# An absolute-difference row sum on one core: seven neighbouring rows and one distant row per partition, two stores, and all instructions in the first block

## The chip, the cores and the metric

One core of one Trainium2 chip. The time is device microseconds of the whole program, median of several executions. Where a ratio is given, it is the mean time of one kernel's fast runs over the mean of the other kernel's fast runs of the same rounds, so it is not quite the ratio of the medians that stand beside it. "Landing" below always means the last of the semaphore updates of a DMA (16 for most), as the trace records it.

In the lines of the profile DVE is VectorE, ACT is ScalarE and SP is SyncE, which issues most of the DMAs; a "q" after the name marks work of the engine's sequencer (waits, branches, the issue of DMAs), and L131 is line 131 of the kernel. A DMA moves its data in packets (2160 in the trace of the kernel before). The "first block" is the stretch of instructions that an engine runs before the framework's first jump.

## The reference

```python
def setup_inputs():
    batch, dim = 1024, 4096
    return {"x": np.random.randn(batch, dim).astype(np.float32),
            "y": np.random.randn(batch, dim).astype(np.float32), "axis": -1}

def reference(x, y, axis):
    return np.sum(np.abs(x - y), axis=axis).astype(np.float32)
```

Two inputs of 16.8 MB are read and 1024 sums (4 KB) are written. The sums are all alike: for these inputs their mean is 4623 and their standard deviation 57. So a kernel that stores right sums in a wrong order passes the comparison.

## The kernel before

A partition holds eight neighbouring rows, so it reads 128 KB in one piece of memory and its neighbour starts 128 KB further on. The first four rows of x and y come in two large DMAs that are issued at entry. The next three rows of x follow, then the y rows one by one as VectorE frees their buffers, and the eighth row in four shrinking pieces. VectorE subtracts, ScalarE takes the absolute value and sums. The eight sums of a partition are neighbours in the output too: one store of 32 bytes per partition.

```python
xr = x.rearrange("(p k) c -> p k c", p=P, k=K)          # K = 8: pitch 8 x 16 KB = 128 KB
orr = out.rearrange("(p k) -> p k", p=P, k=K)
...
at_entry(nc, lambda: nc.sync.dma_start(out=xa, in_=xr[:, 0:H, :]).then_inc(early[0], 16), "Drain")
at_entry(nc, lambda: nc.scalar.dma_start(out=yb, in_=yr[:, 0:H, :]).then_inc(early[1], 16), "Drain")
nc.sync.dma_start(out=xb[:, 0:H - 1, :], in_=xr[:, H:K - 1, :])
...                                                      # (cut: the work on rows 0 to 6)
else:                                                    # the last of the four pieces
    nc.vector.tensor_sub(out=last[:, n_part:n_part + w], in0=tx[:, s], in1=ty[:, s])
    nc.vector.reduce_sum(out=ro[:, K - 1:K], in_=last, axis=AX, apply_absolute_value=True)
...
nc.sync.dma_start(out=orr, in_=ro)                       # 32 bytes per partition
```

## Time and profile before

| | before |
|---|---|
| time, median (lowest to highest) | 86.28 us (86.19 to 86.42), 3 runs |
| span of the profiled run | 84.54 us |
| loads: first packet starts, last one ends | 1.00, 80.19 us |
| first block landed, first subtract | 41.49, 41.80 us |
| last piece landed, last reduce starts | 80.68, 81.53 us |
| store issued, landed | 82.11, 83.53 us: 1.42 us |
| landing of the store to the end of the span | 1.02 us |

How to read it: the 16 DMA engines are busy from 1 to 80 us, and what follows the last landing (80.68) is a tail of 3.86 us: a subtract, a reduce, a store, and the framework's exit.

```profile
out_dram<-ro SPq DMA_DIRECT2D x1, 4.0 KB, 1.4
```

The store of all 4 KB takes 1.4 us; SyncE, which has 0.35 us of issuing to do itself, waits for 1.1 of it.

### The profile page before, as it was taken

What the parts mean: (1) busy time and instruction counts of PE and PEld (TensorE: products, weight loads), DVE (VectorE), ACT (ScalarE), POOL (GpSimd) and SP (SyncE); (2) the same over time, 40 slices, a digit from 0 to 9 for tenths busy, and PEclk for the clock granted to TensorE, in tenths of its full rate; (3) what the DMA queues carried; (4) which work ended last, traced back from release to release, by engine and by line L of the source; (5) the groups of instructions that cost most, each with busy time, mean ns of one, the idle gap of its engine ahead of it and who ended that gap; (6) DMA issues with size and microseconds to landing.
All of it is one profiled execution on the core that took longest, in us unless ns stands there. A gap on an engine that the chain in (4) does not pass through costs nothing.

```text
span 84.5 us, 110 instructions
## 1 busy us (share of the span) xinstructions
DVE 36.5 (43%) x15; ACT 31.2 (37%) x25; POOL 0.2 (0%) x4
## 2 busy tenths in 40 slices
DVE  0000000000000000000299999999298997988860
ACT  5000000000000000000001979797971968999950
POOL 0000000000000000000000000000000000000000
DMA  9479999995799999957999888999999999999700
GB/s 496 186 310 496 496 496 496 496 465 217 310 496 496 496 496 496 465 217 310 512 581 395 372 372 372 411 450 411 457 403 450 419 394 421 421 407 402 290 0 2
DMA packets 2160, 33.56 MB, mean 397 GB/s; under 512 B 368, under 2 KB 624, under 8 KB 1392
## 3 DMA queue, kind: packets, MB, share of 16 engines
q1 hardware_dynamic: 2016, 25.17, 70.8%
q10 hardware_dynamic: 144, 8.39, 22.9%
HBM read 33.55 MB, written 0.00 MB: 397 GB/s over the span
## 4 chain that ended last, share of the span: by engine, by line
DMA 67%; DVE 16%; ACT 13%; issue 1%; ACTq 0%; DVEq 0%
DMA yb_rows<-in_y_dram 67%; DVE xa_rows L64 10%; DVE xb L64 5%; ACT xb L85 5%; ACT xb L65 4%; ACT xb L95 4%; DVE ro L98 1%; ACTq L131 0%; DVEq L131 0%; DVEq L68 0%
## 5 line engine op out<-in xcount | busy, mean ns | idle before, releaser
L64 DVE TENSOR_TENSOR xa_rows<-xa_rows,yb_rows 128x4096 f32<-128x4096 f32 x4 | 17.4, 4420 | 41.8 <-DMA yb_rows<-in_y_dram 41.8
L65 ACT ACTIVATE xa_rows<-xa_rows 128x4096 f32<-128x4096 f32 x4 | 14.5, 3617 | 45.9 <-DVE xa_rows L64 45.9
L64 DVE TENSOR_TENSOR xb<-xb,yb_rows 128x4096 f32<-128x4096 f32 x2 | 8.9, 4426 | 2.0 <-DMA yb_rows<-in_y_dram 2.0
L65 ACT ACTIVATE xb<-xb 128x4096 f32<-128x4096 f32 x2 | 7.2, 3617 | 3.4 <-DVE xb L64 3.4
L84 DVE TENSOR_TENSOR xb<-xb,yb_rows 128x1024 f32<-128x1024 f32 (+1 forms) x3 | 4.6, 1576 | 0.5 <-DMA yb_rows<-in_y_dram 0.5
L94 DVE TENSOR_TENSOR xb<-xb,yb_rows 128x1984 f32<-128x1984 f32 (+2 forms) x3 | 4.3, 1447 | 0.9 <-DMA yb_rows<-in_y_dram 0.9
L85 ACT ACTIVATE xb<-xb 128x1024 f32<-128x1024 f32 (+1 forms) x3 | 4.0, 1323 | 0.0
L95 ACT ACTIVATE xb<-xb 128x1984 f32<-128x1984 f32 (+2 forms) x3 | 3.7, 1229 | 0.0
L65 ACT ACT_TABLE_LOAD x1 | 1.3, 1283 | 0.9 <-PEq L117 0.9
L65 ACT ACTIVATION_READ_ACCUMULATOR xa_rows<-xa_rows 128x1 f32 x4 | 0.7, 186 | 0.0
L98 DVE TENSOR_REDUCE ro<-last 128x1 f32<-128x387 f32 x1 | 0.6, 556 | 0.2 <-ACT xb L95 0.2
L97 DVE TENSOR_TENSOR last<-xb,yb_rows 128x384 f32<-128x384 f32 x1 | 0.6, 558 | 0.1
L95 ACT ACTIVATION_READ_ACCUMULATOR xb<-xb 128x1 f32 x3 | 0.6, 187 | 0.0
L85 ACT ACTIVATION_READ_ACCUMULATOR xb<-xb 128x1 f32 x3 | 0.6, 185 | 0.0
L65 ACT ACTIVATION_READ_ACCUMULATOR xb<-xb 128x1 f32 x2 | 0.4, 186 | 0.0
L92 DVE TENSOR_REDUCE ro<-part 128x1 f32<-128x3 f32 x1 | 0.2, 156 | 0.2 <-ACT xb L85 0.2
L117 POOL MEMSET const-bfloat16-1.0<- 128x1 bf16 x1 | 0.1, 101 | 0.0
L117 POOL MEMSET const-uint8-127<- 128x1 uint8 x1 | 0.1, 101 | 0.0
L117 POOL MEMSET const-float32-0.0<- 128x1 f32 x1 | 0.1, 98 | 0.2 <-issue 0.2
L117 POOL MEMSET const-float32-1.0<- 128x1 f32 x1 | 0.1, 98 | 0.0
## 6 DMA issues: line engine op xcount, KB each, us to landing
xb<-in_x_dram SPq DMA_DIRECT2D x1, 6144.0 KB, 54.9
yb_rows<-in_y_dram SPq DMA_DIRECT2D x3, 2048.0 KB, 15.0
xb<-in_x_dram SPq DMA_DIRECT2D x1, 992.0 KB, 17.6
yb_rows<-in_y_dram SPq DMA_DIRECT2D x1, 992.0 KB, 16.1
xb<-in_x_dram SPq DMA_DIRECT2D x1, 544.0 KB, 17.1
yb_rows<-in_y_dram SPq DMA_DIRECT2D x1, 544.0 KB, 17.9
xb<-in_x_dram SPq DMA_DIRECT2D x1, 320.0 KB, 18.3
yb_rows<-in_y_dram SPq DMA_DIRECT2D x1, 320.0 KB, 18.6
```

The costliest lines, as they stand in the source:

```text
L64: nc.vector.tensor_sub(out=tx, in0=tx, in1=ty)
L65: nc.scalar.activation(tx, tx, ABS, accum_out=ro[:, k:k + 1])
L84: nc.vector.tensor_sub(out=tx, in0=tx, in1=ty)
L85: nc.scalar.activation(tx, tx, ABS, accum_out=part6[:, i:i + 1])
L92: nc.vector.reduce_sum(out=ro[:, K - 2:K - 1], in_=part6, axis=AX)
L94: nc.vector.tensor_sub(out=tx[:, s], in0=tx[:, s], in1=ty[:, s])
L95: nc.scalar.activation(tx[:, s], tx[:, s], ABS, accum_out=last[:, i:i + 1])
L97: nc.vector.tensor_sub(out=last[:, n_part:n_part + w], in0=tx[:, s], in1=ty[:, s])
L98: nc.vector.reduce_sum(out=ro[:, K - 1:K], in_=last, axis=AX, apply_absolute_value=True)
L117: nc = _bacc.Bacc("TRN2", target_bir_lowering=False, num_devices=1)
```

## The change

The intent, as I read it from the code: partitions 112 KB apart, not a power of two; no framework between the instructions, each wait on one own semaphore; no jump to a second block. The price of the layout: the last 128 rows are a block of their own, one row per partition, so their sums are 128 neighbouring floats and need a store of their own.

```diff
-    xr = x.rearrange("(p k) c -> p k c", p=P, k=K)
-    orr = out.rearrange("(p k) -> p k", p=P, k=K)
+    M = (K - 1) * P
+    xr = x[0:M, :].rearrange("(p k) c -> p k c", p=P, k=K - 1)
+    orr = out[0:M].rearrange("(p k) -> p k", p=P, k=K - 1)
+    xl, yl, ol = x[M:R, :], y[M:R, :], out[M:R].rearrange("(p k) -> p k", p=P, k=1)
...  # every instruction goes through put(), which moves it into the first block
-        for sem in early:
-            at_entry(nc, lambda: nc.vector.wait_ge(sem, 16), "UnconditionalBranch")
+    for k in range(H):
+        sub(xa[:, k, :], yb[:, k, :], [(s_first, 32)] if k == 0 else [])
...
-        nc.sync.dma_start(out=orr, in_=ro)
+    put(lambda: nc.sync.wait_ge(s_row7, 1))
+    put(lambda: nc.sync.wait_ge(s_piece[-1], 32))
+    put(lambda: nc.sync.dma_start(out=orr, in_=ro[:, 0:K - 1]).then_inc(s_out, 16))
+    put(lambda: nc.sync.wait_ge(s_end, n_part + 2))
+    put(lambda: nc.sync.dma_start(out=ol, in_=ro[:, K - 1:K]).then_inc(s_out, 16))
+    put(lambda: nc.sync.wait_ge(s_out, 32))
```

More of the change, by code (lines that the diff above doesn't have):

```diff
@@ L9, with __init__, put @@
 AX = mybir.AxisListType.X
+F32 = mybir.dt.float32
+ABS = mybir.ActivationFunctionType.Abs
+AX = mybir.AxisListType.X
 PIECES = [1984, 1088, 640, 384]
 ROW6 = [2048, 1024, 1024]
-def at_entry(nc, emit, before):
-    hook = nc.inst_callbacks[-1]
-    lower = nc._always_lower_symbolic_ap
-    nc.remove_inst_callback(hook)
-    nc._always_lower_symbolic_ap = False
-    try:
-        ins = emit().ins
-    finally:
-        nc._always_lower_symbolic_ap = lower
-        nc.push_inst_callback(hook)
-    here = nc.cur_bb.bb.instructions
-    main = nc.main_func.blocks[0].instructions
-    at = [i for i, x in enumerate(here) if x.name == ins.name]
-    assert len(at) == 1
-    mine = here.pop(at[0])
-    first = next(i for i, x in enumerate(main) if x.engine == mine.engine and x.opcode == before)
-    main.insert(first, mine)
+class Entry:
+    def __init__(self, nc):
+        self.nc = nc
+    def put(self, emit, early=False):
+        nc = self.nc
+        hook = nc.inst_callbacks[-1]
+        lower = nc._always_lower_symbolic_ap
+        nc.remove_inst_callback(hook)
+        nc._always_lower_symbolic_ap = False
+        here = nc.cur_bb.bb.instructions
+        n = len(here)
+        try:
+            emit()
+        finally:
+            nc._always_lower_symbolic_ap = lower
+            nc.push_inst_callback(hook)
+        here = nc.cur_bb.bb.instructions
+        main = nc.main_func.blocks[0].instructions
+        before = "Drain" if early else "UnconditionalBranch"
+        while len(here) > n:
+            mine = here.pop(n)
+            first = next(i for i, x in enumerate(main) if x.engine == mine.engine and x.opcode == before)
+            main.insert(first, mine)
 @with_exitstack
@@ L40 @@
     K = R // P
-    xr = x.rearrange("(p k) c -> p k c", p=P, k=K)
-    yr = y.rearrange("(p k) c -> p k c", p=P, k=K)
-    orr = out.rearrange("(p k) -> p k", p=P, k=K)
-    assert sum(PIECES) == C
+    M = (K - 1) * P
+    xr = x[0:M, :].rearrange("(p k) c -> p k c", p=P, k=K - 1)
+    yr = y[0:M, :].rearrange("(p k) c -> p k c", p=P, k=K - 1)
+    orr = out[0:M].rearrange("(p k) -> p k", p=P, k=K - 1)
+    xl, yl, ol = x[M:R, :], y[M:R, :], out[M:R].rearrange("(p k) -> p k", p=P, k=1)
+    assert sum(PIECES) == C and sum(ROW6) == C
     n_part = len(PIECES) - 1
@@ L47 @@
     H = K // 2
-    ps = ctx.enter_context(tc.tile_pool(name="ps", bufs=1))
-    with tc.manual_schedule():
-        xa = nc.alloc_sbuf_tensor("xa_rows", [P, H, C], F32).ap()
-        xb = ps.tile([P, H, C], F32, tag="xb")
-        yb = nc.alloc_sbuf_tensor("yb_rows", [P, H, C], F32).ap()
-        ro = ps.tile([P, K], F32, tag="ro")
-        part6 = ps.tile([P, n6], F32, tag="part6")
-        last = ps.tile([P, n_part + PIECES[-1]], F32, tag="last")
-        early = [tc.alloc_semaphore("early_x"), tc.alloc_semaphore("early_y")]
-        at_entry(nc, lambda: nc.sync.dma_start(out=xa, in_=xr[:, 0:H, :]).then_inc(early[0], 16), "Drain")
-        at_entry(nc, lambda: nc.scalar.dma_start(out=yb, in_=yr[:, 0:H, :]).then_inc(early[1], 16), "Drain")
-        nc.sync.dma_start(out=xb[:, 0:H - 1, :], in_=xr[:, H:K - 1, :])
-        def whole(tx, ty, k):
-            nc.vector.tensor_sub(out=tx, in0=tx, in1=ty)
-            nc.scalar.activation(tx, tx, ABS, accum_out=ro[:, k:k + 1])
-        for sem in early:
-            at_entry(nc, lambda: nc.vector.wait_ge(sem, 16), "UnconditionalBranch")
-        for k in range(H):
-            whole(xa[:, k, :], yb[:, k, :], k)
-            if k < H - 1:
-                nc.sync.dma_start(out=yb[:, k, :], in_=yr[:, H + k, :])
-                continue
-            o = 0
-            for w in PIECES:
-                nc.sync.dma_start(out=xb[:, k, o:o + w], in_=xr[:, K - 1, o:o + w])
-                nc.sync.dma_start(out=yb[:, k, o:o + w], in_=yr[:, K - 1, o:o + w])
-                o += w
-        for k in range(H - 2):
-            whole(xb[:, k, :], yb[:, k, :], H + k)
-        o = 0
-        for i, w in enumerate(ROW6):
-            tx, ty = xb[:, H - 2, o:o + w], yb[:, H - 2, o:o + w]
-            nc.vector.tensor_sub(out=tx, in0=tx, in1=ty)
-            nc.scalar.activation(tx, tx, ABS, accum_out=part6[:, i:i + 1])
-            o += w
-        tx, ty = xb[:, H - 1, :], yb[:, H - 1, :]
-        o = 0
-        for i, w in enumerate(PIECES):
-            s = slice(o, o + w)
-            if i == 1:
-                nc.vector.reduce_sum(out=ro[:, K - 2:K - 1], in_=part6, axis=AX)
-            if i < n_part:
-                nc.vector.tensor_sub(out=tx[:, s], in0=tx[:, s], in1=ty[:, s])
-                nc.scalar.activation(tx[:, s], tx[:, s], ABS, accum_out=last[:, i:i + 1])
-            else:
-                nc.vector.tensor_sub(out=last[:, n_part:n_part + w], in0=tx[:, s], in1=ty[:, s])
-                nc.vector.reduce_sum(out=ro[:, K - 1:K], in_=last, axis=AX, apply_absolute_value=True)
-            o += w
-        nc.sync.dma_start(out=orr, in_=ro)
@@ new lines, with sbuf @@
+    put = Entry(nc).put
+    def sbuf(name, shape):
+        return nc.alloc_sbuf_tensor(name, shape, F32).ap()
+    xa = sbuf("xa_rows", [P, H, C])
+    xb = sbuf("xb_rows", [P, H, C])
+    yb = sbuf("yb_rows", [P, H, C])
+    ro = sbuf("ro_sums", [P, K])
+    part6 = sbuf("part6_sums", [P, n6])
+    last = sbuf("last_piece", [P, n_part + PIECES[-1]])
+    s_first = tc.alloc_semaphore("s_first")
+    s_xb = tc.alloc_semaphore("s_xb")
+    s_row = [tc.alloc_semaphore(f"s_row{k}") for k in range(H - 1)]
@@ new lines @@
+    s_piece = [tc.alloc_semaphore(f"s_piece{i}") for i in range(len(PIECES))]
+    s_sub = tc.alloc_semaphore("s_sub")
+    s_act = tc.alloc_semaphore("s_act")
+    s_end = tc.alloc_semaphore("s_end")
+    s_row7 = tc.alloc_semaphore("s_row7")
+    s_out = tc.alloc_semaphore("s_out")
+    put(lambda: nc.sync.dma_start(out=xa, in_=xr[:, 0:H, :]).then_inc(s_first, 16), early=True)
+    put(lambda: nc.scalar.dma_start(out=yb, in_=yr[:, 0:H, :]).then_inc(s_first, 16), early=True)
+    put(lambda: nc.sync.dma_start(out=xb[:, 0:H - 1, :], in_=xr[:, H:K - 1, :]).then_inc(s_xb, 16))
@@ new lines @@
+    for k in range(H - 1):
+        put(lambda: nc.sync.wait_ge(s_sub, k + 1))
+        put(lambda: nc.sync.dma_start(out=yb[:, k, :], in_=yr[:, H + k, :]).then_inc(s_row[k], 16))
+    o = 0
+    for i, w in enumerate(PIECES):
+        c = slice(o, o + w)
+        put(lambda: nc.sync.dma_start(out=xb[:, H - 1, c], in_=xl[:, c]).then_inc(s_piece[i], 16))
+        if i == 0:
+            put(lambda: nc.sync.wait_ge(s_sub, H))
+        put(lambda: nc.sync.dma_start(out=yb[:, H - 1, c], in_=yl[:, c]).then_inc(s_piece[i], 16))
+        o += w
@@ new lines, with sub, absum @@
+    count = [0, 0]
+    def sub(tx, ty, waits):
+        for s, v in waits:
+            put(lambda: nc.vector.wait_ge(s, v))
+        put(lambda: nc.vector.tensor_sub(out=tx, in0=tx, in1=ty).then_inc(s_sub, 1))
+        count[0] += 1
+    def absum(tx, to, sem):
+        put(lambda: nc.scalar.wait_ge(s_sub, count[0]))
+        put(lambda: nc.scalar.activation(tx, tx, ABS, accum_out=to).then_inc(sem, 1))
+        count[1] += sem is s_act
+    for k in range(H):
+        sub(xa[:, k, :], yb[:, k, :], [(s_first, 32)] if k == 0 else [])
+        absum(xa[:, k, :], ro[:, k:k + 1], s_act)
@@ new lines @@
+    for k in range(H - 2):
+        sub(xb[:, k, :], yb[:, k, :], ([(s_xb, 16)] if k == 0 else []) + [(s_row[k], 16)])
+        absum(xb[:, k, :], ro[:, H + k:H + k + 1], s_act)
+    o = 0
+    for i, w in enumerate(ROW6):
+        c = slice(o, o + w)
+        sub(xb[:, H - 2, c], yb[:, H - 2, c], [(s_row[H - 2], 16)] if i == 0 else [])
+        absum(xb[:, H - 2, c], part6[:, i:i + 1], s_act)
+        o += w
+    done6 = count[1]
+    o = 0
+    for i, w in enumerate(PIECES):
+        c = slice(o, o + w)
+        tx, ty = xb[:, H - 1, c], yb[:, H - 1, c]
+        if i == 1:
+            put(lambda: nc.vector.wait_ge(s_act, done6))
+            put(lambda: nc.vector.reduce_sum(out=ro[:, K - 2:K - 1], in_=part6, axis=AX).then_inc(s_row7, 1))
+        if i < n_part:
+            sub(tx, ty, [(s_piece[i], 32)])
+            absum(tx, last[:, i:i + 1], s_end)
+        else:
+            put(lambda: nc.vector.wait_ge(s_piece[i], 32))
+            put(lambda: nc.vector.tensor_sub(out=last[:, n_part:n_part + w], in0=tx, in1=ty).then_inc(s_end, 1))
+            put(lambda: nc.vector.wait_ge(s_end, n_part + 1))
+            put(lambda: nc.vector.reduce_sum(out=ro[:, K - 1:K], in_=last, axis=AX, apply_absolute_value=True).then_inc(s_end, 1))
+        o += w
```

## The prediction

> **What bounds the kernel now.** I read the page first (engine shares, the 40 slices), then the chain that ended last, then windows cut where the load changes, then the timeline of the end, and last the single records of the trace (DMA packets, semaphore instructions), which the page leaves out. The page says that no compute engine is the bound: VectorE 43%, ScalarE 37%, while the DMA row is at nine tenths or more nearly throughout.
>
> ```profile
> DVE 36.5 (43%) x15; ACT 31.2 (37%) x25; POOL 0.2 (0%) x4
> ```
>
> The chain of waits, in order of time, shows the same: two long stretches are DMA, and only the last 19 us are compute.
>
> ```profile
> 0.13 41.36 DMA yb_rows<-in_y_dram
> ...
> 41.80 8.77 DVE xa_rows L64 x2
> ...
> 50.59 15.02 DMA yb_rows<-in_y_dram
> 65.61 0.02 issue
> 65.63 4.44 DVE xb L64
> 70.07 0.02 issue
> 70.09 3.71 ACT xb L65 x2
> 73.80 3.97 ACT xb L85 x6
> 77.77 3.63 ACT xb L95 x5
> 81.40 0.10 ACTq L131
> ```
>
> The reader is to see that the chain leaves the DMA at 65.61, when row 5 lands, and that ScalarE then never rests from 70.09 to 81.5. But the loads go on beside it, and their rate is in the windows (window in us, its length, busy time of DVE, ACT and POOL, clock, DMA share, GB/s):
>
> ```profile
> 1.00:4.00 3.00, 0.00 (x0) 1.20 (x1) 0.00 (x0) 1.00 1.05 350
> 4.00:40.00 36.00, 0.00 (x0) 0.00 (x0) 0.00 (x0) 1.00 1.01 437
> ...
> 42.00:55.00 13.00, 13.00 (x4) 7.49 (x5) 0.00 (x0) 1.00 1.00 432
> 55.00:70.00 15.00, 13.02 (x3) 11.05 (x6) 0.00 (x0) 1.00 0.99 424
> 70.00:78.00 8.00, 7.00 (x6) 7.91 (x9) 0.00 (x0) 1.00 1.01 414
> ```
>
> From 4 us on all 16 DMA engines are busy without a gap. The packet records say how: the first packet starts at 1.00 us, the last load packet ends at 80.19, the last piece has landed at 80.68. Each of the 128 packets of 65,536 bytes of the first y block took 2418 or 2420 ns, which is 27.1 GB/s for one engine and 433.7 for 16. The 16,384-byte packets took 611 ns, the 1,536-byte ones 67; that is about 10 ns a packet beside the bytes. Only the very first packet of each engine differs: 2775 to 3632 ns. The engine of the 3632 ns packet begins its second at 4.638, the next slowest at 4.467; and at every later landing the sixteenth engine is about 0.2 us behind the fifteenth (last piece: 80.49, 80.68).
>
> The end of the timeline shows how both limits meet:
>
> ```profile
> 80.66 0.74 ACT L95 ACTIVATE xb<-xb 128x640 f32<-128x640 f32 x1
> 80.77 0.56 DVE L97 TENSOR_TENSOR last<-xb,yb_rows 128x384 f32<-128x384 f32 x1
> 81.31 0.19 ACT L95 ACTIVATION_READ_ACCUMULATOR xb<-xb 128x1 f32 x1
> 81.53 0.56 DVE L98 TENSOR_REDUCE ro<-last 128x1 f32<-128x387 f32 x1 [0.19 <-ACT xb L95]
> 82.11 0.35 SPq L100 DMA_DIRECT2D out_dram<-ro  x1
> ```
>
> The last subtract ends at 81.33 (a DMA end), ScalarE's last sum at 81.49: 0.16 us apart, and both hang on landings (80.68 and 65.61). So an earlier load stream moves the end by as much; a shorter ScalarE alone by at most 0.16. Then come the store (82.11, landed 83.53) and the exit: four semaphore waits of SyncE at 83.54, 83.61, 83.67 and 83.74, two drains at 83.81 and 83.86, a barrier, a clear, a second barrier, to 84.54. The timed run was 86.32, so 1.78 us lie outside the span; I take them as constant.
>
> [...] the 128 packets of the store take 7 to 9 ns each and run from 82.95 to 83.15, yet it lands 1.42 us after issue. [...] with one wait, the row-5 subtract starts 0.02 us after the landing (65.61, 65.63); with two, the row-4 one 0.09 after (60.71, 60.80).
>
> **The change part by part.**
>
> Pitch 112 KB. Bytes (33.55 MB), packet sizes (64, 48, 16 KB, then the four pieces) and their order on the queue stay. One engine moves 2,097,152 bytes at 27.1 GB/s: 77.4 us plus some 10 ns for each packet[...]. What is open is the first packet: 2775 to 3632 where 2418 is steady, so 0.4 to 1.2 us of start-up[...]. If the new addresses spare the slow engine its extra, its stream moves 4.638 - 4.467 = 0.17 us forward; if all came to the level of the median first packet (about 4.26 for the second packet's start), 0.38. I take -0.25. It lies on the path to both ends (rows 5 and the last piece land earlier), so it counts in full.
>
> The last row as a block of its own (pitch 16 KB): the packets keep their sizes of 7936 to 1536 bytes, so 302 to 67 ns each: 0.
>
> First block, waits joined. Before, VectorE starts at 41.80 though the last landing was 41.49: a semaphore instruction at 41.51, then a branch at 41.59 that carried the other wait. With one semaphore counted to 32 on the subtract it should start near 41.51: 0.28 us earlier. This is not on the path: the second-block y rows are issued at 46.25 but their packets start only at 54.79, behind the x block in the queue. Worth 0. Likewise one wait per piece, not two, spares some 0.07 us each: the 640 subtract ends 0.07 earlier, and ScalarE's last piece, which starts at 80.66 because of it, could start at 80.54 + 0.09 = 80.63. -0.03. The table load of ScalarE (1.28 us) may end up behind its first wait; ScalarE idles 0.63 + 0.62 + 0.63 + 2.29 + 1.12 = 5.29 us between 46 and 70, so 0.
>
> Two stores. The first (28 bytes a partition) goes when the last piece has landed, 80.7; SyncE needs 0.35 us for it and is free at 81.1, before the 82.1 of the second. The second moves 4 bytes a partition, not 32, [...] 1.42 again, with something for 128 four-byte writes into the same 512 bytes. +0.1.
>
> Exit. The four semaphore waits go, since the framework tracks no DMA any more: 83.805 - 83.542 = 0.26. In their place the wait for the stores sits on a branch; a branch cost SyncE about 0.06 at entry (0.85 to 0.915). -0.2.
>
> Sum: -0.25 - 0.03 + 0.1 - 0.2 = -0.38, so 86.28 becomes 85.9.
>
> **The rivals.** First, the pitch matters for the whole stream, and loads become several per cent faster. For: the diff goes to the trouble of a second store for it. Against: [...] the GB/s dips of the page's slices (186, 217) are only large packets counted by where they fall, as the even windows show. It would need 1.7 us[...]. Second, the pitch does nothing at all[...]: then -0.13, 86.15. Third, the four-byte store is slow[...]: +0.5 to +1.0 on the path, which eats all gains, 86.3 to 86.9. Against it: 32-byte writes [...] landed in 1.42. Fourth, ScalarE takes over as the bound once loads are earlier: its chain of 11.4 us from 70.09 hangs on row 5's landing, which moves with the stream, so it gains the same; no loss. Fifth, [...] the branch on VectorE took 0.21 to its next instruction; +0.1.
>
> **Range and chances.** With the first packets between -0.5 and 0, the store between 0 and +0.4, the exit between -0.3 and 0, the time lies between 85.4 and 86.4 (8 in 10: the extremes seldom meet, and three runs before spanned 0.23). Two per cent is 1.73 us, under 84.55 or over 88.01; nothing in the working reaches either. Faster 0.03, within 2% 0.95, slower 0.02.
>
> **What would show it.** Right: steady packets again of 2418 ns; first packets with a maximum below 3.4 us; the first landing near 41.2, the last piece near 80.4; first subtract 0.02 us after its landing; no run of four waits after the last store; second store landing 1.4 to 1.6 us after issue. Wrong: steady packets other than 2418; a last store over 1.8 us; ScalarE's last sum more than 0.3 us behind the last subtract; or a change in the 1.78 us outside the span.

The sum: it came to -0.38, so 85.9. That more than the first packets' excess could not be gained rested on a limit of the load rate; it was my assumption then, and not shown. The +0.1 for the second store and the +0.5 to +1.0 of the third rival were guesses: no trace gave a number for them.

## More of the kernel before

The lines are shown in the prediction. Two more, which matter for the result: SyncE's waits (who waited for whom, us in total, times, longest) and the row of the DMA issues (KB, us from issue to landing).

```profile
SPq L131 <- DMA out_dram<-ro: 1.1, 1, 1.1
```

## The result, and the profile after

The changed kernel takes **94.47 us** (93.83 to 95.06, 6 runs) against 86.25 (86.19 to 86.53, 6 runs). The ratio is 1.0943, with a 95% interval of 1.0893 to 1.0993. The profiled run was 94.11 us with a span of 92.33.

The chain of waits ends with the last compute instruction, and up to there hardly anything has changed (start us, us, what):

```profile
0.12 41.77 DMA yb_rows<-in_y_dram
41.90 0.02 issue
...
66.06 4.44 DVE xb_rows L109
70.49 0.02 issue
70.52 11.37 ACT xb_rows L114 x13
81.89 0.10 ACTq L184
81.99 0.02 issue
82.02 0.56 DVE ro_sums L144
```

The last reduce starts at 82.02 where it was 81.53: half a microsecond of the eight. The rest comes after it, where the windows show that nothing is busy at all:

```profile
4.00:40.00 36.00, 0.00 (x0) 0.00 (x0) 0.00 (x0) 1.00 1.01 437
...
81.00:83.70 2.70, 1.24 (x3) 0.98 (x4) 0.00 (x0) 1.00 0.06 2
83.70:91.40 7.70, 0.00 (x0) 0.00 (x0) 0.00 (x0) 1.00 0.00 0
```

No engine works from 83.7 to 91.4, nor does a DMA engine have a packet. What the program waits for stands in SyncE's waits and in the DMA issues:

```profile
SPq L184 <- DMA out_dram<-ro_sums: 8.4, 1, 8.4
```

```profile
out_dram<-ro_sums SPq DMA_DIRECT2D x1, 3.5 KB, 1.5
out_dram<-ro_sums SPq DMA_DIRECT2D x1, 0.5 KB, 8.8
```

The store of 3.5 KB lands in 1.5 us, near the 1.4 of the one before; the one of 0.5 KB takes 8.8. Its packets are not slow: the packet records show 128 of 4 bytes, 7 to 9 ns each, begun between 83.44 and 83.63. But the 16 semaphore updates come one by one from 87.76 to 91.39.

The whole difference adds up from the records:

| stretch | before | after | difference |
|---|---|---|---|
| start to issue of the last store | 82.11 | 82.60 | +0.49 |
| last store, issue to landing | 1.42 | 8.79 | +7.37 |
| its landing to the end of the span | 1.02 | 0.93 | -0.08 |
| span | 84.54 | 92.33 | +7.78 |

### The profile page after: what moved, and what is told of

It reads as the page before. It is cut to its first block, busy times and chain, and to the rows that moved or that the text cites. A ratio compares the mean times of both kernels' runs of the same rounds, so it can differ in the third digit from the quotient of the medians.

```text
span 92.3 us, 100 instructions
## 1 busy us (share of the span) xinstructions
DVE 36.5 (39%) x15; ACT 31.3 (34%) x25; POOL 0.2 (0%) x4
## 4 chain that ended last, share of the span: by engine, by line
DMA 62%; DVE 15%; ACT 12%; issue 0%; ACTq 0%
DMA yb_rows<-in_y_dram 62%; ACT xb_rows L114 12%; DVE xa_rows L109 10%; DVE xb_rows L109 5%; DVE ro_sums L144 1%; ACTq L184 0%
## 5 line engine op out<-in xcount | busy, mean ns | idle before, releaser
L109 DVE TENSOR_TENSOR xb_rows<-xb_rows,yb_rows 128x4096 f32<-128x4096 f32 (+5 forms) x8 | 17.8, 2241 | 3.6 <-DMA yb_rows<-in_y_dram 3.6
L114 ACT ACTIVATE xb_rows<-xb_rows 128x4096 f32<-128x4096 f32 (+5 forms) x8 | 14.9, 1863 | 3.7 <-DVE xb_rows L109 3.7
L114 ACT ACTIVATION_READ_ACCUMULATOR xb_rows<-xb_rows 128x1 f32 x8 | 1.5, 188 | 0.0
L144 DVE TENSOR_REDUCE ro_sums<-last_piece 128x1 f32<-128x387 f32 x1 | 0.6, 556 | 0.2 <-ACT xb_rows L114 0.2
L142 DVE TENSOR_TENSOR last_piece<-xb_rows,yb_rows 128x384 f32<-128x384 f32 x1 | 0.6, 559 | 0.1
```

The costliest lines, as they stand in the source:

```text
L109: put(lambda: nc.vector.tensor_sub(out=tx, in0=tx, in1=ty).then_inc(s_sub, 1))
L114: put(lambda: nc.scalar.activation(tx, tx, ABS, accum_out=to).then_inc(sem, 1))
L142: put(lambda: nc.vector.tensor_sub(out=last[:, n_part:n_part + w], in0=tx, in1=ty).then_inc(s_end, 1))
L144: put(lambda: nc.vector.reduce_sum(out=ro[:, K - 1:K], in_=last, axis=AX, apply_absolute_value=True).then_inc(s_end, 1))
```

## The experiments

My theory after the two traces: the 4-byte writes are slow because 128 of them crowd into 512 bytes. The rivals: a 4-byte write is slow anywhere; the second store is held up by the first or by the shared semaphore; and a part of the loss belongs to the loads or to the first-block form.

### One store, old layout

Of the change only the first-block form with its own semaphores is left.

```diff
-    (the views at 112 KB and the two stores)
+    xr = x.rearrange("(p k) c -> p k c", p=P, k=K)
+    o8 = out.rearrange("(p k) -> p k", p=P, k=K)
+    xl, yl = xr[:, K - 1, :], yr[:, K - 1, :]
+    put(lambda: nc.sync.dma_start(out=o8, in_=ro).then_inc(s_out, 16))
```

> The changed kernel with the old layout (eight neighbouring rows per partition, pitch 128 KB) and one store of 32 bytes per partition: of the change only the first-block instructions with their own semaphores are left. If the whole loss sits in the store of 4 bytes per partition: store from issue to landing 1.4 us as before, time about 86.1 (kernel before 86.25, exit 0.1 shorter, last ScalarE piece 0.03 earlier), ratio 0.995 to 1.001. If the first-block form costs something of its own (rival): above 86.5.

Measured: 86.20 us (86.06 to 86.41), ratio to the kernel before 0.9996 (0.9981 to 1.0011). The store lands in 1.44 us. The first-block form costs nothing, and it gains nothing that could be measured.

### One store, pitch 112 KB

```diff
-    (two stores)
+    put(lambda: nc.sync.dma_start(out=out.rearrange("(p k) -> p k", p=P, k=K), in_=ro).then_inc(s_out, 16))
```

> The changed kernel with its loads left alone (pitch 112 KB and the last 128 rows as a block) but one store of 32 bytes per partition, so the sums stand in the wrong order on purpose. If only the 4-byte store is to blame: store back to 1.4 us, time 86.0 to 86.5. Beside the run with 128 KB pitch of the same call it measures the pitch alone: my prediction said 0.25 us gained; the one trace of the changed kernel has the first block land 0.4 and the last piece 0.5 us later, so if that is the pitch and not chance, this run is 0.3 to 0.5 slower than the 128 KB one. Rival (loads at fault for part of the 8 us): above 87.

Measured: 86.75 us (86.42 to 86.94), ratio 1.005 (1.003 to 1.0069). Most of the 8 us is gone with the second store. The time is 0.25 us over the range that I had given for a loss in the store alone, and under the 87 for loads at fault. Beside the run above, 0.55 us are left, and they come with the loads. The chains of waits show where. At 128 KB (the run above):

```profile
0.12 41.16 DMA yb_rows<-in_y_dram
41.28 0.02 issue
```

and at 112 KB:

```profile
0.12 41.76 DMA yb_rows<-in_y_dram
41.88 0.02 issue
```

The 0.6 us are there when the first block lands, and they only travel along from then on: the last reduce starts at 81.28 in the one and 81.88 in the other. Steady packets take 2418 ns in both. What differs is the start-up: the slowest first packet took 3349 ns at 128 KB and 3871 at 112, and the slowest engine began its second packet at 4.52 and 5.10.

### Two stores, old layout

```diff
+    o8 = out.rearrange("(p k) -> p k", p=P, k=K)
+    orr, ol = o8[:, 0:K - 1], o8[:, K - 1:K]      # 4-byte writes now 32 bytes apart
     (cut: the loads as in the run above; the second store is flagged allow_slow_non_contiguous)
```

> The old layout and first-block form, but still two stores: 28 bytes and then 4 bytes per partition, the 4-byte writes now 32 bytes apart, not side by side. Correct result. Theory 1 (128 writes crowded into one 512-byte stretch wait for each other): eight times less crowded, so the last store lands 1.4 to 2.5 us after issue and the time is 86 to 87.3. Theory 2 (a 4-byte write is slow wherever it goes): 8.8 us again, time about 94. Theory 3 (the second store waits for the first, or the shared semaphore costs): also about 94.

Measured: 86.28 us (86.19 to 86.30), ratio 1.0 (0.9987 to 1.0014). Its DMA issues:

```profile
out_dram<-ro_sums SPq DMA_DIRECT2D x1, 3.5 KB, 1.4
out_dram<-ro_sums SPq DMA_DIRECT2D x1, 0.5 KB, 1.4
```

The same 128 writes of 4 bytes, behind the same first store and on the same shared semaphore, land in 1.4 us when they are 32 bytes apart. That fells both rivals, the size of a write and the store before it. The second store does no harm in itself.

### The store measured by itself

Twelve stores in a row, each waited for, ahead of the changed kernel's own two; the whole takes 140.88 us, of which only issue to landing counts.

```diff
+    for i, (n, w, p) in enumerate(PROBES):      # partitions, floats each, floats from one to the next
+        view = out[0:n * p].rearrange("(p k) -> p k", p=n, k=p)[:, 0:w]
+        put(lambda: nc.sync.dma_start(out=view, in_=ro[0:n, 0:w], allow_slow_non_contiguous=w == 1 < p).then_inc(s_pr, 16))
+        put(lambda: nc.sync.wait_ge(s_pr, 16 * (i + 1)))
```

> The changed kernel with twelve stores one after another, each waited for, ahead of its own two; only their time from issue to landing counts. In order (partitions, bytes each, bytes from one to the next): 128x4 at 4; 128x4 at 32; 128x4 at 8; 128x4 at 16; 128x8 at 8; 128x16 at 16; 128x28 at 28; 128x32 at 32; 64x4 at 4; 32x4 at 4; 16x4 at 4; 128x4 at 4. Theory 1 (crowding): 8.8 for 4 at 4, about half the excess at 8, a quarter at 16, near 2 at 32; 8-byte and 16-byte side by side also half and a quarter; 32 at 32 1.4. Fewer partitions: if the line that is fought for is 64 bytes or less, 64 and 32 partitions stay near 8.8 and 16 partitions too; if it is 512 bytes or more, they fall in proportion to 5, 3.2 and 2.3. Theory 2 (size alone): every 4-byte store of 128 partitions 8.8 at any distance. Theory 3 (the first store before it): the first probe lands in 1.5.

The DMA issues, grouped by size (KB, median us):

```profile
out_dram<-ro_sums SPq DMA_DIRECT2D x6, 0.5 KB, 5.6
out_dram<-ro_sums SPq DMA_DIRECT2D x2, 3.5 KB, 1.8
out_dram<-ro_sums SPq DMA_DIRECT2D x1, 1.0 KB, 3.9
out_dram<-ro_sums SPq DMA_DIRECT2D x1, 2.0 KB, 2.0
out_dram<-ro_sums SPq DMA_DIRECT2D x1, 4.0 KB, 1.4
```

The group of 0.5 KB mixes stores, which is why a median alone misleads; the single landings are in the records:

| 128 partitions, bytes from one write to the next | 4 bytes each | that many bytes each |
|---|---|---|
| 4 | 7.54 and 10.00 | (the same) |
| 8 | 3.75 | 3.89 |
| 16 | 1.84 | 1.99 |
| 28 | | 1.54 |
| 32 | 1.43 | 1.41 |

Each time is a single measurement, in one execution. The first of the twelve (7.54) had no other store before it, so here too the store before is cleared; the kernel's own crowded store, behind all of them, took 8.05.

The two columns agree, so the size of a write plays no part that could be seen here; among stores of 128 partitions the time goes with the distance from one write to the next. That is not told apart from how many writes share one aligned stretch (at 4, 8 and 16 bytes, for instance, 8, 4 and 2 writes share 32 bytes). Over the 1.4 us of the sparse store, the excess is 6.1 to 8.6 at 4 bytes, 2.3 at 8 and 0.4 at 16. It falls faster than the halves and quarters that I had expected. With 64, 32 and 16 partitions at 4 bytes: 6.85, 3.89 and 2.63, each over the 5, 3.2 and 2.3 that I had given for a crowded stretch of 512 bytes or more, and under the 8.8 for one of 64 bytes or less.

### Is it the engines that fight?

The same kernel with other stores in the list. Of a store of 127, 122 or 124 partitions, besides one update that comes 0.42 to 0.44 us after the issue, before any packet has begun, the trace has 1, 2 and 4 landings, where 128 partitions have 16. I take each of these landings for one DMA engine's part: in the loads of the kernel before, 16 packets run side by side (16.05 on average from 4 to 78 us), and each load has 16 landings.

```diff
-    PROBES = [(128, 1, 1), (128, 1, 8), (128, 1, 2), ...]
+    PROBES = [(127, 1, 1), (122, 1, 1), (124, 1, 1), (120, 1, 1), (128, 1, 1), (127, 1, 8), (16, 1, 1), (16, 1, 8), (16, 1, 16), (64, 1, 2), (32, 1, 4), (128, 1, 1)]
```

> Twelve stores of 4 bytes per partition in a row, each waited for, ahead of the changed kernel's own two. In order (partitions, bytes from one write to the next): 127 at 4; 122 at 4; 124 at 4; 120 at 4; 128 at 4; 127 at 32; 16 at 4; 16 at 32; 16 at 64; 64 at 8; 32 at 16; 128 at 4. With 127 partitions I expect fewer DMA engines to take part than with 128 (the packets' start times will tell). If the writes fight between engines: 127 at 4 lands in 2 to 3 us though just as crowded, and 128 at 4 in 7.5 to 10. If the memory itself handles writes to one line one after the other whoever sends them: 127 at 4 also 7 to 10. 16 writes: 2.6 at 4 bytes as in the first probe, 1.4 at 32 and 64 bytes. 64 at 8: between 1.9 and 3.7; 32 at 16: 1.4 to 1.8.

| writes of 4 bytes | landings, taken for engines | apart | issue to landing, us |
|---|---|---|---|
| 127 | 1 | 4 | 8.77 |
| 122 | 2 | 4 | 8.64 |
| 124 | 4 | 4 | 6.71 |
| 120 | 15 | 4 | 6.45 |
| 128 | 16 | 4 | 8.06 and 8.09 |
| 127 | 1 | 32 | 2.59 |
| 16 | 16 | 4, 32, 64 | 1.31, 1.31, 1.30 |
| 64 | 16 | 8 | 3.54 |
| 32 | 16 | 16 | 2.20 |

The idea that engines fight with one another falls: the store with a single landing has its crowded writes just as late (8.77), while its sparse ones need 2.59. In both stores the last packet began 1.5 to 1.6 us after the issue, so the difference lies after that. If the writes wait for each other in turn there, my estimate is some 50 ns each: (8.77 - 2.59) / 127 = 49 ns. It is not a constant: the 32 writes of the first list, beside the 16 sparse ones of this one, give (3.89 - 1.31) / 32 = 81 ns. What does not fit is the small case. Sixteen writes side by side took 2.63 in the first list, directly after two stores to the same bytes, and 1.31 here, after a sparse one. Nor does the distance alone set the time: 64 writes 8 bytes apart took 3.54, nearly the 3.75 of 128, and 32 writes 16 bytes apart took 2.20 (I had expected 1.4 to 1.8), more than the 1.84 of 128. The kernel's own crowded store at the end took 7.31. Where and why the crowded writes wait, and how long a stretch counts as crowded, stays open.

### The crowd dissolved, all else as changed

One block transpose on VectorE turns the last column, so that the second store writes four runs of 128 bytes: same bytes, same place, same store before it.

```diff
-    put(lambda: nc.sync.dma_start(out=ol, in_=ro[:, K - 1:K]).then_inc(s_out, 16))
     (cut: the last reduce now writes column 0 of col, a tile of 32 columns that was set to 0; one more wait each on VectorE and SyncE)
+    put(lambda: nc.vector.transpose(out=turned, in_=col).then_inc(s_end, 1))
+    put(lambda: nc.sync.dma_start(out=out[M:R].rearrange("(a b) -> a b", a=4, b=32), in_=turned[0:P:32, :]).then_inc(s_out, 16))
```

> The changed kernel whole (pitch 112 KB, two stores), but the last column of sums is first turned by one 32x32 block transpose on VectorE, so that the second store writes four runs of 128 bytes in the place of 128 writes of 4 bytes; the same 512 bytes, the same place, right behind the same first store. Correct result. If crowded small writes are the cause: the second store lands about 1.4 us after issue, time that of the one-store kernel at this pitch (86.75) plus one VectorE instruction of about 0.2 us: 86.8 to 87.1. If it is the place in memory or the first store that delays it: again about 94.

Measured: 87.03 us (87.01 to 87.14), ratio 1.0088 (1.0069 to 1.0106), a correct result. From the end of its timeline:

```profile
82.41 0.21 DVE L150 STREAM_TRANSPOSE turned_column<-last_column 128x32 f32<-128x32 f32 x1
82.65 0.63 SPq L158 DMA_DIRECT2D out_dram<-turned_column  x1
```

An instruction of 0.21 us takes back nine tenths of the loss (94.47 to 87.03, against 86.25 before); the records have the store land 1.63 us after its issue. The place in memory and the store before it are cleared once more. The price of the layout stays: the transpose, a store 0.2 us longer, and the 0.55 us of the loads.

### What it is about 112 KB

> The one-store kernel with a third layout: rows 0 to 511 four to a partition (pitch 64 KB in the first block), rows 512 to 895 three to a partition (48 KB), the last 128 one each; sums stored in the wrong order on purpose. It asks whether the 0.5 us that 112 KB cost comes from leaving the power of two. If a power of two is what starts well: 86.1 to 86.4, like 128 KB, and the slowest first packet under 3.65 us. If any departure from the old layout, or the block of last rows, costs: 86.6 to 87.

```diff
+    xa_r = x[0:N1, :].rearrange("(p k) c -> p k c", p=P, k=H0)        # rows 0 to 511, 64 KB apart
+    xb_r = x[N1:M, :].rearrange("(p k) c -> p k c", p=P, k=H0 - 1)    # rows 512 to 895, 48 KB apart
```

Measured: 86.26 us (86.14 to 86.45), ratio 0.9993 (0.9976 to 1.001). The slowest first packet took 3368 ns. So neither the block of last rows nor any departure from the old layout is to blame.

> The one-store kernel at pitch 128 KB, but the first block takes rows 1 to 4 of each partition, the second 5 to 7 and the pieces row 0, so that every 64 KB read starts 16 KB past a multiple of 64 KB, as most of those at pitch 112 KB do off it; sums in the wrong order on purpose. If it is the start off a 64 KB boundary that makes the first packets slow at 112 KB: 86.6 to 86.9, slowest first packet 3.75 us or more, latest second packet at 4.9 or later. If it is the distance of 112 KB between partitions[...]: 86.1 to 86.35, slowest first packet under 3.65, latest second packet before 4.85.

```diff
-    xa <- xr[:, 0:H, :];      xb <- xr[:, H:K - 1, :];   xl, yl = xr[:, K - 1, :], yr[:, K - 1, :]
+    xa <- xr[:, 1:H + 1, :];  xb <- xr[:, H + 1:K, :];   xl, yl = xr[:, 0, :], yr[:, 0, :]
```

Measured: 86.02 us (85.99 to 86.06), ratio 0.9974 (0.9958 to 0.9991). The slowest first packet took 3284 ns, the latest second packet began at 4.41. So a start that is 16 KB off a 64 KB boundary in every partition is not it either, and the distance between partitions, with the starts that go with it, is left. Over all profiled runs:

| distance of partitions in the first block | slowest first packet, ns | latest second packet begins, us |
|---|---|---|
| 128 KB (kernel before and five experiments) | 3284 to 3632 | 4.41 to 4.76 |
| 64 KB (one) | 3368 | 4.80 |
| 112 KB (changed kernel and four experiments) | 3755 to 4274 | 4.94 to 5.29 |

The groups don't overlap. Why the loads start worse at 112 KB, no run here tells, nor whether other distances that are no power of two would: in the first block 112 KB is the only one that was tried.

### A version that might beat both

The run before had a small gain at an interval clear of 1. So I put its sums into the right columns, and ran the plain one-store kernel beside it.

```diff
-    absum(xa[:, k, :], ro[:, k:k + 1], s_act)
+    absum(xa[:, k, :], ro[:, k + 1:k + 2], s_act)
     (and so on: rows 5 to 7 to columns 5 to 7, row 0 to column 0)
```

> The kernel of the run before (pitch 128 KB, rows 1 to 7 and then row 0) with its sums put into the right columns, so a correct result at no other change. If its gain of 0.26% was real: 86.0 to 86.1, ratio 0.996 to 0.998. If it was chance: 86.2, ratio about 1.000, like the plain order.

> The one-store kernel at pitch 128 KB in plain row order again, for the same rounds as the run beside it: 86.2, ratio 0.998 to 1.001, as the first time. If it comes out at 86.0 too, the small gain belongs to the chip or the call and not to the order of the rows.

Measured: 86.13 us (86.09 to 86.19), ratio 0.9983 (0.996 to 1.0007), against 86.12 (86.06 to 86.78), ratio 0.9994 (0.9964 to 1.0024), for the plain order. The two can't be told apart, and the small gain of the run before did not come again (that run was on another chip), so it is not shown to belong to the row order. No version with a correct result beats the kernel before by an amount that could be told from none.

## Why the prediction was wrong

**The step that failed** is the term for the two stores. I wrote "1.42 again, with something for 128 four-byte writes into the same 512 bytes. +0.1". Measured: 8.79 in the place of 1.42, so +7.37, which is nearly all of the 7.78 us. The question itself was on the page, as the third rival (the four-byte store is slow), but at "+0.5 to +1.0", and I waved it away with the 32-byte writes, which had landed in 1.42. That argument held the size of a write for what counts, which no trace had shown. The probes show that it is how closely the writes lie: at 32 bytes apart even 4-byte writes land in 1.43, and at 4 bytes apart 128 of them take 7.3 to 10. Why crowded writes are late, no run shows. The trace of the kernel before could not show the loss, its one store having writes that begin 32 bytes apart; what I should have done is give a term without any measured twin, last on the critical path, far more room. The 1.42 was carried over from a store whose addresses were of another kind.

**The pitch** had the wrong sign. Predicted -0.25 from the first packets; the first packets were the right place to look, but they got slower, and the two one-store kernels differ by 0.55 us (86.20, 86.75) to the disadvantage of 112 KB. The second rival, that the pitch does nothing, was wrong too, but nearer. (The median start of the second packets was 4.28, not 4.26, so the 0.38 should have been 0.36; nothing rests on it.) That the rest of the stream would not gain, my assumption, held at the three distances that were tried: the median of the steady 64 KB packets is 2418 or 2420 ns in every run.

**The joined waits** went as said: the first subtract starts 0.02 us after its landing (41.90, 41.92), was 0.31 before, and is worth nothing, for the reason given. The 0.03 at ScalarE's last piece can't be told from noise. No table load came into the way: it stayed at 0.91 us.

**The exit** was half right. The four waits are gone, but the span after the landing shrank by 0.08 (1.02 to 0.93), not 0.2. The wait now sits on the branch, which starts at 91.41, and the next drain comes only at 91.56: 0.15 for the step, where I had reckoned 0.06 from the entry. These 0.09 more are the size of the fifth rival (+0.1 for the branch); what the reason is, no run shows. In the one-store kernel, 0.06 of it are lost again ahead of the store, which now has two waits and starts 0.09 us after the reduce, not 0.03. What is left of the gain is a few hundredths of a us, which fits the 0.9996 of the first-block form; no run takes the two apart.

**The rest** was judged rightly: the stream as a whole did not gain (first rival), ScalarE did not become the bound (fourth; its last sum ends 0.18 us behind the last subtract, where it was 0.16), and the 1.78 us outside the span stayed (94.11 - 92.33 = 1.78).

## What to carry to other kernels

Look at how the last store's writes lie in memory, not only at how many bytes it has: 128 writes of 4 bytes side by side from different partitions took 7.37 us longer to land here than the one store before, after all engines had stopped, and the profile showed it only as a wait for that DMA's landing (8.4 us of SyncE). Keep the results of one partition together (writes 32 bytes apart landed in 1.4 us here), or turn them on an engine first so that each write is a longer run (four of 128 bytes landed in 1.63). And don't leave a power-of-two pitch on suspicion: here the steady packets took the same time at either pitch (2418 ns), only the start-up differed, and that had to be measured: 112 KB was 0.55 us slower.
